# Sliding-window attention of a hybrid layer: the score scale applied where the mask is added, and four heads normalised by one product with a broadcast reciprocal

## Chip, cores and metric

The kernel runs on one core of a Trainium2 chip. The metric is the device time of one execution in microseconds (us); lower is better. The engines are named as in the profile: PE (TensorE, matrix products), PEld (its weight loads), DVE (VectorE), ACT (ScalarE), POOL (GpSimd) and SP (SyncE, which issues nearly all DMAs here).

## What is computed

One layer of a streaming encoder on 2048 tokens of 1024 columns: a token mixing block (one input projection whose columns feed 8 heads of sliding attention and 4 heads of a gated linear recurrence, HGRN2; one output projection), then cross-attention into 256 memory tokens, then a SwiGLU FFN. The change lies in the sliding attention alone:

```python
s = jnp.einsum('bnqhgd,bnkhd->bnhgqk', qc, kband).astype(jnp.float32) * (Dh ** -0.5)   # Dh = 64
s = jnp.where(valid[None, :, None, None, None, :], s, NEG_INF)
sink = ...                                # one learned logit for each head
p = jax.nn.softmax(jnp.concatenate([s, sink], axis=-1), axis=-1)[..., :L]
o = jnp.einsum('bnhgqk,bnkhd->bnqhgd', p.astype(v.dtype), vband)
```

A chunk of 64 queries reads its own chunk of keys and the two before it. The 8 query heads share 2 key heads, 4 and 4.

## The kernel before

All products run in 32-bit reduced form, each operand split into a high and a low part, so that a product is two or three matmuls. The work is staged: the input projection of the first 1024 tokens (up to about 255 us), then a stage of about 350 us in which three things are interleaved, then a passage of some 150 us that prepares the cross-attention weights (`fold_cross`) beside the second half of the recurrence, then the long products of the output projection, the cross-attention and the FFN.

The stage in the middle is the one that matters here. `mix` (line 194) advances generators in turn: `swa` (964, the sliding attention, 16 tiles of 128 tokens), `hgrn` (946, the recurrence) and `in_proj` (682, the input projection of the second 1024 tokens, one block of 128 columns at a step). What the generators emit is not the order of the engines: the kernel is built with a scheduler (`schedule_with_timeline_sim=True`) that reorders the whole instruction stream by its own forecast of durations and then fixes one queue for each engine. Each engine works through its queue in order, so an instruction that waits holds all that stand behind it. A changed instruction can therefore move others that the change doesn't touch.

For each tile, `swa_front` (754) does this. It loads the queries of 4 heads twice, into partitions 0 to 63 and 64 to 127 of `qd`; ACT makes `qs` with its scale (768) and DVE replaces the lower half by the remainder (769). Keys are split into `kh` and `kl` (779). A head's scores are two matmuls (803, 804) into a PSUM bank that holds two heads. One DVE instruction (808) adds the mask to the scores, writes the sum to `S` and leaves the row's minimum; ACT takes the exponential with that minimum and leaves the row's sum (812). For 4 heads together POOL adds the sink to the minimum (815), ACT takes its exponential (816), POOL adds it to the sums (818), DVE takes the reciprocal (820), and four DVE products, one for each head, multiply `S` by its column of the reciprocal (821 to 823). As the scores enter with a minus sign (the queries are scaled by -0.125), minima stand for maxima and the mask is +1e30.

`swa_back` (826) works one tile later: PE transposes `S` (837), ACT and DVE split the result into `pth` (841) and `ptl` (842), PE multiplies by the values (846, 847), ACT and DVE gather the halves into `ys` (850, 851), and `ys` is stored.

Some other lines take part in the argument. `in_cols` (690) loads a block of `w_in` columns into `raw`, splits it into `whi` and `wlo`, multiplies (156 to 158 into `psg`), ends a gate block with DVE (711) and stores `z` to `z_d` (721). The `z` tiles have two buffers. After the last block the same two buffers serve the prologue of `phases` (1317 to 1321): pieces of `w_out` are loaded into `z` and split into the resident tiles `T` by ACT (985) and DVE (988). `hgrn_front` (854) loads `k1`, `qq`, `kk`, `v` from `z_d`, and PE transposes `kk` (895) and `v` (900). `fold_cross` (272) transposes the memory tokens (124), and ACT and DVE write `mT` (126, 127) for the products that follow.

Of the kernel before, what the change touches and what calls it, by code (L numbers as in the profile page):

```python
# [11 lines left out]
F32 = mybir.dt.float32  # L12
F32R = mybir.dt.float32r
I32 = mybir.dt.int32
AF = mybir.ActivationFunctionType
ALU = mybir.AluOpType
AX = mybir.AxisListType

P = 128
T = 2048  # L20
D = 1024
M = 256
# [9 lines left out]
BIG = 1e30  # L32
# [4 lines left out]
def f32(ap):  # L37
    return ap.bitcast(F32)
# [10 lines left out]
class Layer:  # L49
# [345 lines left out]
    def zero_tiles(self):  # L395
        nc, ph = self.nc, self.hg

        self.wmask = self.sw.tile([P, M], F32, name="wmask")
        nc.vector.memset(self.wmask, 0.0)
        nc.vector.memset(self.wmask[0:64, 192:256], BIG)  # L400
        nc.vector.memset(self.wmask[64:128, 0:64], BIG)

        cm = self.io.tile([P, P], F32, tag="u", name="cm", bufs=2)
        nc.vector.memset(cm, 1.0)
        nc.gpsimd.affine_select(cm, cm, [[1, P]], ALU.is_ge, 0.0, base=0, channel_multiplier=-1)
        nc.vector.memset(cm[0:64, 64:128], 0.0)
        self.cmask = ph.tile([P, P], I32, name="cmask")
        nc.vector.tensor_copy(self.cmask, cm)

        self.atz = []  # L410
        for i in range(2):
            a = ph.tile([P, 4, P], F32, name=f"atz{i}")
            nc.gpsimd.memset(a, 0.0)
            self.atz.append(a)
        self.vst_prev = None
        self.W = ph.tile([P, 4, P], F32, tag="W", name="W0", bufs=2)
        nc.gpsimd.memset(self.W, 0.0)
# [336 lines left out]
    def swa_front(self, n, kinds):  # L754
        nc, ph = self.nc, self.sw
        t0 = n * P
        z = self.z_d
        nk = 2 if n else 1
        kinds = itertools.cycle(kinds)

        qs = []
        for g in range(2):
            qd = ph.tile([P, 4, P], F32, tag="qd", name=f"qd{n}_{g}", bufs=2)
            qsrc = z[g * 256:(g + 1) * 256, t0:t0 + P].rearrange("(h d) t -> d h t", d=64)
            self.load(qd[0:64], qsrc)
            self.load(qd[64:128], qsrc)
            q = ph.tile([P, 4, P], F32R, tag="qs", name=f"qs{n}_{g}", bufs=2)
            nc.scalar.activation(q, qd, AF.Copy, scale=-0.125)
            nc.vector.scalar_tensor_tensor(q[64:128], qd[64:128], -0.125, f32(q[64:128]), ALU.mult, ALU.subtract)
            qs.append(q)  # L770

        kr = ph.tile([P, 2, M], F32, tag="kr", name=f"kr{n}")
        kl = ph.tile([P, 2, M], F32R, tag="kl", name=f"kl{n}")
        kh = ph.tile([P, 2, M], F32R, tag="kh", name=f"kh{n}")
        o = M - nk * P
        ksrc = z[C_KA:C_VA, t0 + P - nk * P:t0 + P].rearrange("(g d) t -> d g t", d=64)
        self.load(kr[0:64, :, o:], ksrc)
        self.load(kr[64:128, :, o:], ksrc)
        self.split(kr[:, :, o:], kh[:, :, o:], kl[:, :, o:])

        vr = ph.tile([P, P], F32, tag="vr", name=f"vr{n}")
        self.load(vr, z[C_VA:C_QH, t0:t0 + P])
        pv = self.bank(next(kinds))
        nc.tensor.transpose(pv[:, 0:P], vr, self.ident)
        vst = ph.tile([P, 2, P], F32R, tag="vst", name=f"vst{n}", bufs=3)
        nc.scalar.activation(vst[:, 0, 0:64], pv[:, 0:64], AF.Copy)
        nc.scalar.activation(vst[:, 1, 64:128], pv[:, 64:128], AF.Copy)
        nc.vector.tensor_tensor(vst[:, 0, 64:128], pv[:, 0:64], f32(vst[:, 0, 0:64]), ALU.subtract)
        nc.vector.tensor_tensor(vst[:, 1, 0:64], pv[:, 64:128], f32(vst[:, 1, 64:128]), ALU.subtract)
        vs = [vst] if nk == 1 else [self.vst_prev, vst]  # L790
        self.vst_prev = vst

        S = []
        for g in range(2):
            mn = self.small("w_mn", 4)
            den = self.small("w_den", 4)
            for i2 in range(2):
                s = ph.tile([P, 2, M], F32, tag="S", name=f"S{n}_{g}{i2}", bufs=6)
                S.append(s)
                ps = self.bank(next(kinds))  # L800
                for r in range(2):
                    pr = ps[:, r * M + o:(r + 1) * M]
                    nc.tensor.matmul(pr, qs[g][:, 2 * i2 + r, :], kh[:, g, o:], start=True, stop=False)
                    nc.tensor.matmul(pr, qs[g][:, 2 * i2 + r, :], kl[:, g, o:], start=False, stop=True)
                for r in range(2):
                    i = 2 * i2 + r
                    h = 4 * g + i
                    nc.vector.tensor_tensor_reduce(  # L808
                        out=s[:, r, o:], in0=ps[:, r * M + o:(r + 1) * M], in1=self.wmask[:, o:],
                        op0=ALU.add, op1=ALU.min, scale=1.0, scalar=self.nsink[:, h:h + 1],  # L810
                        accum_out=mn[:, i:i + 1])
                    nc.scalar.activation(s[:, r, o:], s[:, r, o:], AF.Exp, bias=mn[:, i:i + 1], scale=-1.0,  # L812
                                         accum_out=den[:, i:i + 1])
            se = self.small("w_se", 4)
            nc.gpsimd.tensor_tensor(se, self.sink[:, 4 * g:4 * g + 4], mn, ALU.add)
            nc.scalar.activation(se, se, AF.Exp)
            dn = self.small("w_dn", 4)
            nc.gpsimd.tensor_tensor(dn, den, se, ALU.add)
            rd = self.small("w_rd", 4)
            nc.vector.reciprocal(rd, dn)  # L820
            for i in range(4):
                a = S[2 * g + i // 2][:, i % 2, o:]
                nc.vector.tensor_scalar_mul(a, a, rd[:, i:i + 1])
        return S, vs

    def swa_back(self, n, kinds, S, vs):
        nc, ph = self.nc, self.sw
        nk = len(vs)
        o = M - nk * P
        kinds = itertools.cycle(kinds)  # L830
        ys = ph.tile([P, 4, P], F32, tag="ys", name=f"ys{n}")
        for g in range(2):
            t = []
            for kb in range(nk):
                ps = self.bank(next(kinds))
                for i in range(4):
                    nc.tensor.transpose(ps[:, i * P:(i + 1) * P],  # L837
                                        S[2 * g + i // 2][:, i % 2, o + kb * P:o + (kb + 1) * P], self.ident)
                th = ph.tile([P, 512], F32R, tag="pth", name=f"pth{n}_{g}{kb}", bufs=3)
                tl = ph.tile([P, 512], F32R, tag="ptl", name=f"ptl{n}_{g}{kb}", bufs=2)  # L840
                nc.scalar.activation(th, ps, AF.Copy)
                nc.vector.tensor_tensor(tl, ps, f32(th), ALU.subtract)
                t.append((th, tl))
            ps = self.bank(next(kinds))
            for kb in range(nk):
                nc.tensor.matmul(ps, vs[kb][:, g, :], t[kb][0], start=(kb == 0), stop=False)
                nc.tensor.matmul(ps, vs[kb][:, g, :], t[kb][1], start=False, stop=(kb == nk - 1))
            a, c = (slice(0, 64), slice(64, 128)) if g == 0 else (slice(64, 128), slice(0, 64))
            pr = ps.rearrange("p (h t) -> p h t", h=4)
            nc.scalar.activation(ys[a], pr[c], AF.Copy)  # L850
            nc.vector.tensor_tensor(ys[a], pr[a], ys[a], ALU.add)
        self.store(self.y_d[n, :, 0:512], ys.rearrange("p k t -> p (k t)"))
# [902 lines left out]
```

## Time and profile before

| | |
|---|---|
| time, median of 3 runs | 2589.82 us (2588.64 to 2592.41) |
| span of the profiled execution, first to last instruction | 2585.7 us |
| median less that span | 4.1 us |
| PE busy | 2548.3 us of the span (99%) |
| DVE busy | 1747.9 us (68%) |
| ACT busy | 1261.0 us (49%) |
| POOL busy | 428.4 us (17%) |
| mean granted TensorE clock | 0.998 |

The profile is of one execution. Its span leaves out what lies before the first and after the last instruction; the 4.1 us is the distance from that span to the median of the timed runs. A matmul's busy time runs on past the start of the next (0.39 us long, started every 0.23 us), so that a PE that is "busy" may still lose a tenth of a microsecond here and there. The four 128x256 products of line 823 run from 285.6 to 605.2 us of the span, and all of the sliding attention lies between about 277 and 625 us.

### The profile page before, as it was taken

The page shows a single profiled execution, that of the slowest core. Times are in us where ns is not written, and L with a number is a line of the kernel's source. Part 1 is how long each engine was busy: PE and PEld are TensorE (multiplying, and loading weights), DVE is VectorE, ACT ScalarE, POOL GpSimd, SP SyncE. Part 2 cuts the span into 40 slices and gives each one's busy share as a digit, 9 for nine tenths or more (in the row PEclk, how much of TensorE's full clock was granted, in tenths as well). Part 3 has the DMA queues.
Part 4 walks back from the last instruction along what each step waited for, and adds up shares of the span by engine and source line. Part 5 has one row for each costly group of instructions (what it writes and reads, how often), then busy time and mean ns, then how long its engine had stood idle before and what let it go on. Part 6 is the DMA issues. An engine that isn't in the chain of part 4 may idle for free.

```text
span 2585.7 us, 34998 instructions
## 1 busy us (share of the span) xinstructions
PE 2548.3 (99%) x12371; PEld 2135.9 (83%) x12371; DVE 1747.9 (68%) x2759; ACT 1261.0 (49%) x2633; POOL 428.4 (17%) x612
## 2 busy tenths in 40 slices
PE   9999999999999999999999999999999999999998
PEld 8888888888988778888878888888888888888886
DVE  7785588986557778788876655576566556564656
ACT  5563466665555566465563333353333334443543
POOL 5231334321302232222300000000000000000022
PEclk9999999999999999999999999999999999999999
DMA  6445655855888886666963622253565444566888
GB/s 188 147 163 179 198 168 152 253 185 167 258 290 281 296 287 210 205 222 210 327 233 115 203 97 75 98 203 124 177 205 194 146 146 139 208 201 186 262 213 218
DMA packets 363663, 506.03 MB, mean 196 GB/s; under 512 B 20960, under 2 KB 249312, under 8 KB 363488
## 3 DMA queue, kind: packets, MB, share of 16 engines
q1 hardware_dynamic: 357440, 481.77, 56.5%
q0 software_dynamic: 6048, 22.02, 4.7%
q8 instruction: 97, 1.59, 0.2%
q14 instruction: 78, 0.64, 0.1%
HBM read 337.00 MB, written 166.72 MB: 195 GB/s over the span
## 4 chain that ended last, share of the span: by engine, by line
PE 83%; DMA 7%; DVE 4%; ACT 3%; issue 2%; POOL 1%; SPq 0%; DVEq 0%; POOLq 0%; ACTq 0%
PE psm L1122 23%; PE psm L1124 23%; PE psm L1123 22%; PE psg L156 2%; PE psg L157 2%; PE psg L158 2%; PE pss L1374 1%; DMA row<-y_d 1%; DMA raw<-in_wo_x_dram 1%; DMA u_d<-row 1%; DMA h1t_d<-row 1%; DMA row<-h_d 1%; ACT junk L1471 1%; ACT T L985 0%; PE pss L837 0%
## 5 line engine op out<-in xcount | busy, mean ns | idle before, releaser
L1122 PE MATMUL psm<-T,S 128*128 128x512 f32 x2695 | 1043.8, 391 | 11.0 <-ACT part L1137 6.5
L1123 PE MATMUL psm<-T,S 128*128 128x512 f32 x2695 | 1049.1, 390 | 2.1 <-DVE T L988 1.9
L1124 PE MATMUL psm<-T,S 128*128 128x512 f32 x2695 | 1038.9, 390 | 3.6 <-DVE S L988 3.6
L1122 PEld LDWEIGHTS psm<-T,S 128*128 128x128 f32 x2695 | 506.2, 188 | 120.3 <-ACT part L1137 7.0
L1124 PEld LDWEIGHTS psm<-T,S 128*128 128x128 f32 x2695 | 506.2, 188 | 110.4 <-DVE S L988 5.3
L1123 PEld LDWEIGHTS psm<-T,S 128*128 128x128 f32 x2695 | 506.5, 188 | 107.5 <-DVE T L988 4.1
L985 ACT ACTIVATE S<-sum 128x512 fp32r<-128x512 f32 (+1 forms) x314 | 188.7, 619 | 359.6 <-PE psm L1124 267.8
L988 DVE TENSOR_TENSOR S<-sraw,S 128x512 fp32r<-128x512 f32 (+1 forms) x319 | 217.0, 687 | 215.9 <-ACT S L985 201.8
L988 DVE TENSOR_TENSOR S<-sum,S 128x512 fp32r<-128x512 f32 (+1 forms) x372 | 249.7, 681 | 47.0 <-ACT S L985 31.8
L1137 ACT ACTIVATE part<-psm 128x512 f32<-128x512 f32 x273 | 161.7, 597 | 242.8 <-PE psm L1124 221.5
L985 ACT ACTIVATE S<-sraw 128x512 fp32r<-128x512 f32 (+1 forms) x272 | 167.4, 617 | 111.2 <-PE psm L1124 99.3
L1500 POOL DMA_DIRECT2D row<-y_d x28 | 25.7, 919 | 1111.4 <-DVE row L1686 1036.5
L988 DVE TENSOR_TENSOR T<-row,T 128x1024 fp32r<-128x1024 f32 (+1 forms) x120 | 141.3, 1192 | 60.9 <-ACT T L985 60.4
L1471 ACT ACTIVATE junk<-row 128x512 f32<-128x512 f32 x160 | 99.7, 625 | 60.5 <-DVE row L1493 30.0
L157 PE MATMUL psg<-u,whi 128*128 128x512 f32 x320 | 127.8, 399 | 0.0
L158 PE MATMUL psg<-u,wlo 128*128 128x512 f32 x320 | 127.1, 397 | 0.0
L156 PE MATMUL psg<-u,whi 128*128 128x512 f32 x320 | 127.1, 397 | 0.0
L985 ACT ACTIVATE T<-row 128x1024 fp32r<-128x1024 f32 x120 | 119.9, 1028 | 10.5 <-DMA row<-qk_s 3.5
L987 POOL TENSOR_SCALAR S<-sum 128x512 fp32r<-128x512 f32 x58 | 53.4, 921 | 294.6 <-PE psm L1124 237.2
L1637 DVE TENSOR_TENSOR row<-psm,part 128x512 f32<-128x512 f32 x66 | 43.7, 687 | 61.4 <-PE psm L1124 61.3
L1646 DVE TENSOR_TENSOR part<-psm,part 128x512 f32<-128x512 f32 x60 | 39.7, 687 | 62.4 <-PE psm L1124 62.2
L812 ACT ACTIVATE S<-S,w_mn 128x256 f32<-128x256 f32 (+1 forms) x128 | 63.1, 495 | 28.6 <-DVE w_mn L808 28.3
(363 smaller groups left out, 3679.1 us busy)
## 6 DMA issues: line engine op xcount, KB each, us to landing
sraw<-in_w_gate_dram SPq DMA_DIRECT2D x44, 512.0 KB, 3.7
sraw<-in_w_up_dram SPq DMA_DIRECT2D x44, 512.0 KB, 3.7
hid_d<-row SPq DMA_DIRECT2D x44, 512.0 KB, 2.7
h_d<-row SPq DMA_DIRECT2D x32, 512.0 KB, 4.8
y_d<-row SPq DMA_DIRECT2D x32, 512.0 KB, 3.3
sraw<-hid_d SPq DMA_DIRECT2D x32, 512.0 KB, 5.1
row<-y_d POOLq DMA_DIRECT2D x28, 512.0 KB, 7.1
sraw<-in_w_in_dram SPq DMA_DIRECT2D x44, 256.0 KB, 3.5
```

Source lines behind the costliest of these rows:

```text
L156: nc.tensor.matmul(ps, ah, bh, start=(i == 0), stop=False)
L157: nc.tensor.matmul(ps, ah, bl, start=False, stop=False)
L158: nc.tensor.matmul(ps, al, bh, start=False, stop=(i == n - 1))
L812: nc.scalar.activation(s[:, r, o:], s[:, r, o:], AF.Exp, bias=mn[:, i:i + 1], scale=-1.0, accum_out=den[:, i:i + 1])
L985: self.nc.scalar.activation(hi, raw, AF.Copy)
L987: self.nc.gpsimd.tensor_scalar(hi, raw, 1.0, 1.0, ALU.mult, ALU.mult)
L988: self.nc.vector.tensor_tensor(lo, raw, f32(hi), ALU.subtract)
L1122: nc.tensor.matmul(ps, s[:, 0, k, :], t[:, 0, k, :], start=st, stop=False, **kw)
L1123: nc.tensor.matmul(ps, s[:, 0, k, :], t[:, 1, k, :], start=False, stop=False, **kw)
L1124: nc.tensor.matmul(ps, s[:, 1, k, :], t[:, 0, k, :], start=False, stop=sp, **kw)
L1137: nc.scalar.activation(t, ps, AF.Copy)
L1471: self.nc.scalar.activation(junk, a, AF.Square, scale=float(D) ** -0.5, accum_out=to)
```

## The change

Three edits, all in the sliding attention:

- The queries are no longer scaled: `qs` is a plain copy, and its lower half is a plain subtraction (a tensor_tensor in place of a scalar_tensor_tensor). The mask becomes -1e30, and the instruction that adds it multiplies the sum by -0.125, with an argument that it has already (`scale`, 1.0 before).
- `S` is one tile of four heads with three buffers in place of tiles of two heads with six buffers; the bytes are the same.
- The four products of a group of heads with their columns of the reciprocal become one tensor_tensor of 128x1024 (128x512 in the first tile of tokens, which has half the keys), whose second operand is the 128x4 reciprocal repeated along the keys. There are 32 such groups.

```diff
         nc.vector.memset(self.wmask, 0.0)
-        nc.vector.memset(self.wmask[0:64, 192:256], BIG)
-        nc.vector.memset(self.wmask[64:128, 0:64], BIG)
+        nc.vector.memset(self.wmask[0:64, 192:256], -BIG)
+        nc.vector.memset(self.wmask[64:128, 0:64], -BIG)
...
             q = ph.tile([P, 4, P], F32R, tag="qs", name=f"qs{n}_{g}", bufs=2)
-            nc.scalar.activation(q, qd, AF.Copy, scale=-0.125)
-            nc.vector.scalar_tensor_tensor(q[64:128], qd[64:128], -0.125, f32(q[64:128]), ALU.mult, ALU.subtract)
+            nc.scalar.activation(q, qd, AF.Copy)
+            nc.vector.tensor_tensor(q[64:128], qd[64:128], f32(q[64:128]), ALU.subtract)
...
             den = self.small("w_den", 4)
+            s4 = ph.tile([P, 4, M], F32, tag="S", name=f"S{n}_{g}", bufs=3)
+            S.append(s4)
             for i2 in range(2):
-                s = ph.tile([P, 2, M], F32, tag="S", name=f"S{n}_{g}{i2}", bufs=6)
-                S.append(s)
+                s = s4[:, 2 * i2:2 * i2 + 2, :]
...
                     nc.vector.tensor_tensor_reduce(
                         out=s[:, r, o:], in0=ps[:, r * M + o:(r + 1) * M], in1=self.wmask[:, o:],
-                        op0=ALU.add, op1=ALU.min, scale=1.0, scalar=self.nsink[:, h:h + 1],
+                        op0=ALU.add, op1=ALU.min, scale=-0.125, scalar=self.nsink[:, h:h + 1],
                         accum_out=mn[:, i:i + 1])
...
             nc.vector.reciprocal(rd, dn)
-            for i in range(4):
-                a = S[2 * g + i // 2][:, i % 2, o:]
-                nc.vector.tensor_scalar_mul(a, a, rd[:, i:i + 1])
+            a = s4[:, :, o:]
+            nc.vector.tensor_tensor(a, a, rd.unsqueeze(2).broadcast_to([P, 4, nk * P]), ALU.mult)
...
                     nc.tensor.transpose(ps[:, i * P:(i + 1) * P],
-                                        S[2 * g + i // 2][:, i % 2, o + kb * P:o + (kb + 1) * P], self.ident)
+                                        S[g][:, i, o + kb * P:o + (kb + 1) * P], self.ident)
```

In the built program DVE's queue loses 96 instructions (128 products become 32); PE, ACT, POOL and SP keep their counts. The scheduler gives another order, too: on all five engines the queues differ from the second tile of the sliding attention on to the end of the passage after it. Before that they agree, and behind it too, but for a few neighbours that change places.

## Prediction

> **What bounds the kernel now.** I read the page first: its span, the line of PE in part 1, and the chain that ended last.
>
> ```profile
> span 2585.7 us, 34998 instructions
> PE 2548.3 (99%) x12371; PEld 2135.9 (83%) x12371; DVE 1747.9 (68%) x2759; ACT 1261.0 (49%) x2633; POOL 428.4 (17%) x612
> PE 83%; DMA 7%; DVE 4%; ACT 3%; issue 2%; POOL 1%; SPq 0%; DVEq 0%; POOLq 0%; ACTq 0%
> ```
>
> PE is busy 99% of the span and makes 83% of the chain; DVE makes 4% of it. The change leaves PE's 12371 matmuls as they are, and works on DVE. Whether DVE matters in the stage at hand is told by the busy time in stretches, then by PE's waits in the sliding attention (255 to 605 us) and in the passage behind it (605 to 650 us).
>
> ```profile
> core 0: us, PE busy (x) PEld busy (x) DVE busy (x) ACT busy (x) POOL busy (x), PEclk, DMA share, GB/s
> 255.00:605.00 350.00, 348.04 (x1927) 297.21 (x1926) 278.11 (x693) 207.18 (x606) 118.55 (x187) 1.00 0.63 189
> 605.00:650.00 45.00, 41.62 (x266) 37.54 (x265) 28.07 (x41) 24.84 (x46) 5.04 (x7) 0.96 0.69 194
> ```
> ```profile
> PE psh L847 <- DVE ptl L842: 0.9, 3, 0.5
> PE pss L803 <- DVE vst L789: 0.5, 1, 0.5
> PE pst L837 <- DVE w_mn L808: 0.2, 1, 0.2
> ```
> ```profile
> PE pst L900 <- DMA v<-z_d: 1.7, 1, 1.7
> PE psg L895 <- issue: 1.2, 1, 1.2
> PE pst L923 <- ACT atz L886: 0.5, 1, 0.5
> ```
>
> In the stage of the change PE is idle 350.00 - 348.04 = 2.0 us, of which it waited 0.9 + 0.5 + 0.2 = 1.6 us for DVE. That is all that a faster DVE can win there. In the 45 us behind it PE is idle 3.4 us and its clock is granted at 0.96, worth another 45 x 0.04 = 1.8 us; the largest wait is for a DMA, the load of `v`.
>
> **The change part by part.** First the product itself. These groups are from the view by line and shape within 255 to 605 us (count, busy us, mean ns); the last row is from the view of line 738, the tensor_tensor 128x1024 with a repeated operand that the kernel has already (min, median, max ns).
>
> ```profile
> L823 DVE TENSOR_SCALAR S<-S,w_rd 128x256 f32<-128x256 f32 x119 | 37.1, 374 | 1.3
> L823 DVE TENSOR_SCALAR S<-S,w_rd 128x128 f32<-128x128 f32 x8 | 2.5, 382 | 0.1
> L769 DVE SCALAR_TENSOR_TENSOR qs<-qd,qs 64x512 fp32r<-64x512 f32 x32 | 25.7, 804 | 10.2 <-ACT qs L768 9.4
> L842 DVE TENSOR_TENSOR ptl<-pst,pth 128x512 fp32r<-128x512 f32 x27 | 18.4, 680 | 3.6 <-PE pss L847 1.6 <-ACT pth L841 1.1 <-PE psg L158 1.0
> L738 DVE TENSOR_TENSOR u<-u,d_mid 128x1024 f32<-128x1024 f32 x4 | 4.9, 1217 | 0.0
> L738 DVE TENSOR_TENSOR pair<-pair,d_mid x4: 1211/1218/1628, 110.9 to 175.2; 128x1024 f32<-128x1024 f32 x4
> ```
>
> Removed: 127 of the 128 products, 37.1 + 2.5 = 39.6 us. Added: 30 products of 128x1024 and 2 of 128x512. By line 738's mean of 1.217 us and line 842's of 0.680 us that is 30 x 1.217 + 2 x 0.680 = 37.9 us; if all were as slow as line 738's slowest (1.628 us), 50.2 us. So DVE gains 1.7 us or loses up to 10.6 us over 345 us. I take -1.7 us, since the mean of one group of line 738 and the median of the other agree at 1.217 and 1.218 us.
>
> The last of the four old products ended 1.13 us after the first began (next fence, second row), so the group is ready 0.1 us later. No new wait appears: the reciprocal already needs the sums of all four heads, so the first old product too stood behind four exponentials. The transposes need all four heads anyway.
>
> The subtraction on line 769 keeps its shape and its two operands in SBUF; its time is bounded by line 842's 0.680 us and its own 0.804 us, a gain of 0 to 32 x 0.124 = 4.0 us on DVE; I take 0. The copy on ACT, the mask, and the scale in line 808 change a constant: 0. The three buffers of `S` hold the same three groups as the six did: 0.
>
> All this is on DVE, and PE waited 1.6 us for DVE in the stage. The cover is what stands between in PE's queue: the input projection's matmuls. In the built queue 8.1 us of PE work or more (by the matmuls' own starting distances) separates a group's last score from its first transpose before the change, and 11.6 us or more after it. So the direct part is worth between -1.6 us and, if PE's waits for DVE doubled, +1.6 us; I take 0.
>
> ```profile
> 300.15 1.39 DVE L823 TENSOR_SCALAR S<-S,w_rd 128x256 f32<-128x256 f32 x4
> 583.81 1.14 DVE L823 TENSOR_SCALAR S<-S,w_rd 128x256 f32<-128x256 f32 x4
> ```
> ```profile
> 300.00 0.62 POOL L987 TENSOR_SCALAR kh<-kr 128x512 fp32r<-128x512 f32 x1 [1.03 <-PE pss L804]
> ```
>
> Those are four old products beside a POOL instruction (1.39 us) and without one (1.14 us). The Trainium skill, page "SBUF — State Buffer", section "Who interferes with whom", says that DVE and GpSimd hold a shared pair of ports for a whole instruction, the later one blocked, and that a DVE instruction with two SBUF inputs contends with GpSimd's reads. By that rule the new product is no freer than the old ones, which the two rows bear out, and it holds POOL out for 1.2 us in one piece. That would put a price on DVE and POOL, which the rival below works out.
>
> **Second, the order.** This is where I see a cost. The chain that ended last, from 608 to 632 us (start, us, what), and then SP's, PE's and ACT's rows that belong to it:
>
> ```profile
> 606.66 0.44 PE pss L837 x4
> 608.91 0.25 PE psg L157
> 609.19 1.07 ACT whi L985
> 612.73 3.87 DMA z_d<-z
> 617.27 4.08 DMA z<-in_w_out_dram
> 621.43 1.07 ACT T L985
> 622.53 1.24 DVE T L988
> 623.78 0.61 SPq L75
> 624.45 5.09 DMA z<-in_w_out_dram
> 630.59 1.55 ACT mT L126 x3
> ```
> ```profile
> 625.10 0.59 SPq L75 DMA_DIRECT2D v<-z_d  x1
> ```
> ```profile
> 630.19 0.63 PE L900 MATMUL pst<-ident,v 128*128 128x128 f32 x4 [1.71 <-DMA v<-z_d]
> 630.65 0.82 PE L884 MATMUL psg<-qq,k 128*128 128x192 f32 x4
> 632.65 0.63 PE L895 MATMUL psg<-ident,kk 128*128 128x128 f32 x4 [1.18 <-issue]
> 633.77 0.49 PE L923 MATMUL pst<-vt,atz 128*128 128x128 f32 x2 [0.49 <-ACT atz L886]
> ```
>
> The end of a projection block releases ACT's `whi`, then a gate tile is finished and stored, its `z` buffer takes a piece of `w_out` (4.08 us), ACT and DVE split that, and only then does SP issue the next piece and, behind it, `v` for tile 9. PE wants that `v` at 628.5 us and gets it at 630.19. In the queues of the changed kernel three things differ.
>
> (a) The block that starts the chain ends earlier: 16 transposes (0.11 us each) and 4 matmuls of 512 columns (0.23 us) that stood ahead of its last matmul now stand behind it: 16 x 0.11 + 4 x 0.23 = 2.7 us earlier.
>
> (b) `v` for tile 9 now stands behind one more piece of `w_out` on SP, which waits for the split of the one before. The piece that was issued at 623.78 goes out at 621.1; it lands at 621.1 + 0.6 + 5.1 = 626.8; ACT 1.07 and DVE 1.24 give 629.2 with their gaps; one issue of 0.6 us gives `v` at 629.9 in place of 625.10; after the same 630.19 - 625.10 = 5.1 us, line 900 starts at 635.0 in place of 630.19: +4.8 us.
>
> (c) Given back: products of line 884 (0.65 us to the next start at full clock) and line 895 (0.44) that stood behind the wait now stand ahead of it, and their own waits of 1.18 and 0.49 us fall into the longer one: 2.8 us. Lost again: ACT now makes the four `mT` copies behind the squares of line 928, which need line 923's result. Three copies are 1.55 us, to which I add about 1.0 us for the squares and 0.6 us on DVE (estimates; a DVE instruction of 512 columns is 0.68 above); against 2.5 us of PE work that stands between, 0.7 us is left over.
>
> Sum of the order: +4.8 - 2.8 + 0.7 = +2.7 us. Its bounds: if `v` costs nothing more than before, -3.4 us (this passage's idle time gone) with -1.8 us for the clock; if nothing is given back and the clock is held low twice as long, 4.8 + 0.7 + 1.8 = +7.3 us, with up to 2 us more in the next passage.
>
> The whole: 0 + 2.7. Against the profiled span that is 2588.4 us; the median of the runs lies 4.1 us above that span, so 2589.8 + 2.7 = 2592.5 us.
>
> **The rivals.**
>
> *Slower by the order.* The mechanism is (b) at its full price: PE meets `v` late and nothing is given back, because the chain does not start 2.7 us early. For it: the late load is the largest wait there now, and every step of the chain is a row. Against it: the work moved ahead. It decides when `v` is issued later than about 631 us. Time: 2589.8 + 7.3 = 2597.1 us.
>
> *Slower by the shared port.* POOL is busy 118.55 of 350 us, 34%; if each of the 32 products then waits half of its own 1.2 us, that is 32 x 0.34 x 0.6 = 6.5 us on DVE and as much on POOL. For it: the row of 1.39 us. Against it: DVE's idle time in the stage is 72 us, PE's wait for it 1.6 us. It decides if all of it reaches PE: 2596.3 us. This is what the skill's rule above would give.
>
> *Faster.* The new order removes the waits: 2.0 us of the stage, 3.4 us behind it and 1.8 us of clock, together 7.2 us: 2582.6 us. For it: transposes keep more distance, and the chain starts earlier. Against it: one more `w_out` piece ahead of `v`.
>
> **How the numbers follow.** A measurement of this kernel can tell about 0.2% (5.2 us) from no change. Forecast, with its own range of 2587 to 2595 us: 0.47. Slower by the order 0.29, by the port 0.06, faster 0.18. So: faster by over 0.2% 0.18, within 0.2% 0.47, slower 0.35. The range of 8 in 10 goes from the faster rival, 2582.5, to the slower one and its 2 us in the next passage with a little room for the runs' own scatter of 2588.64 to 2592.41: 2601 us.
>
> **What would show it.** Right: 32 rows on line 823 of about 1.22 us (0.69 for two), DVE's sum on that line near 38 us, PE busy about 348 of 350 us in the stage, and the wait of line 900 for `v` grown from 1.7 us to 3 us or more. Wrong: products of 1.5 us or more; PE waiting for lines 823 or 842 by several us; `v` for tile 9 landing before PE reaches it; or a new wait in the rest of the stage, whose order I judged by the distances in the queues alone.

## The result, and the profile after

| | before | after |
|---|---|---|
| time, median of 6 runs each | 2591.93 us (2588.64 to 2594.0) | 2599.53 us (2597.02 to 2602.69) |
| ratio after / before, 95% interval | | 1.003 (1.0019 to 1.004) |
| span of the profiled execution | 2585.7 us | 2600.6 us |

The changed kernel is 7.6 us slower, 0.3%. The forecast was 2592.5 us and "within 0.2%"; the measured time is outside the likeliest case's own range (2587 to 2595 us) and inside the whole one. It was forecast as +2.7 us with 0.47 for "within 0.2%" and 0.35 for "slower": the way was right, the size was not, and the range held because it was wide. The profiled execution after took 2602.3 us in all, 1.7 us more than its span, and is one of the slowest of its six; the two profiled spans are 14.9 us apart, twice the medians, so a difference between two single profiles is read below only where it comes back in other runs.

The page of the changed kernel: its span, the line of PE in part 1, and the chain that ended last.

```profile
span 2600.6 us, 34912 instructions
PE 2551.2 (98%) x12371; PEld 2137.4 (82%) x12371; DVE 1750.0 (67%) x2663; ACT 1260.9 (48%) x2633; POOL 438.5 (17%) x612
PE 79%; DMA 8%; DVE 4%; ACT 3%; issue 2%; POOL 2%; SPq 1%; DVEq 0%; POOLq 0%; ACTq 0%
```

DVE's busy time has hardly moved (1747.9 and 1750.0 us) and POOL's has grown by 10 us; PE has lost a point of its share, and the chain of waits has given four points from PE to the others. Where PE lost it is told by the busy time in stretches, after, with the same columns as before:

```profile
255.00:605.00 350.00, 344.17 (x1913) 294.91 (x1912) 274.24 (x585) 204.09 (x595) 127.51 (x185) 1.00 0.65 189
605.00:650.00 45.00, 40.01 (x237) 35.00 (x236) 29.43 (x46) 23.74 (x51) 6.04 (x9) 0.96 0.63 165
650.00:715.00 65.00, 57.89 (x473) 55.72 (x473) 30.32 (x47) 30.83 (x82) 19.66 (x25) 1.00 0.84 235
```

and, before, the third stretch, which the prediction did not show:

```profile
650.00:715.00 65.00, 63.72 (x533) 62.77 (x532) 30.68 (x50) 33.58 (x96) 23.05 (x29) 1.00 0.82 255
```

PE's idle time (length less busy) in the stage is 5.8 us where it was 2.0; in 605 to 650 us 5.0 where it was 3.4; in 650 to 715 us 7.1 where it was 1.3. The groups of the changed lines on DVE in 255 to 650 us:

```profile
L823 DVE TENSOR_TENSOR S<-S,w_rd 128x1024 f32<-128x1024 f32 x30 | 37.9, 1268 | 1.5
L823 DVE TENSOR_TENSOR S<-S,w_rd 128x512 f32<-128x512 f32 x2 | 1.9, 960 | 0.2
L769 DVE TENSOR_TENSOR qs<-qd,qs 64x512 fp32r<-64x512 f32 x32 | 23.3, 732 | 8.9 <-ACT qs L768 8.0
```

The product itself is near what the prediction said (37.9 us): 32 rows with a sum of 39.8 us, against 37.4 + 2.5 us for the old ones in the same window. So DVE's time on it does not explain PE's new idle time. What PE waited for (total us, times, longest), in the stage and in 605 to 800 us:

```profile
PE pss L837 <- DVE vst L789: 1.7, 1, 1.7
PE pst L837 <- DVE ys L851: 0.9, 1, 0.9
PE psh L804 <- DVE sg L942: 0.8, 1, 0.8
PE pst L837 <- DVE w_mn L809: 0.7, 1, 0.7
PE pss L837 <- DVE w_mn L809: 0.6, 1, 0.6
```
```profile
PE pst L900 <- DVE on L933: 3.3, 1, 3.3
PE pst L884 <- ACT atz L886: 3.0, 1, 3.0
PE psg L884 <- POOL h_vv L930: 1.6, 1, 1.6
PE psh L156 <- ACT whi L985: 1.5, 1, 1.5
```

Only the two waits for line 809 (808 before), the instruction with the new scale, are for a line that the change touches, and with the old scale in the same order, in old_in_new_order below, they are longer (1.2 and 1.0 us). The two largest that came back in the other runs of this order have the same shape; the wait for line 933, 3.3 us here, is 0.4 and 1.0 us in two others. Late in the stage (first fence, DVE and then PE, start and us) DVE stands 6.74 us before a sum of `w_out` blocks whose load has not landed, and behind it stand the values `vst` for which PE's bank is held. In the passage (second fence, ACT; third, PE) ACT stands 3.52 us before the split of a `w_out` piece; the copy of `atz`, ready since DVE's line 885 (626.92 us, 0.43 us), stands behind it and two more, and PE waits 2.96 us.

```profile
527.93 1.22 DVE L1032 TENSOR_TENSOR u<-u,x 128x1024 f32<-128x1024 f32 x1 [6.74 <-DMA x<-in_w_out_dram]
```
```profile
629.80 1.06 ACT L985 ACTIVATE T<-z 128x1024 fp32r<-128x1024 f32 x1 [3.52 <-DMA z<-in_w_out_dram]
632.32 0.26 ACT L886 ACTIVATE atz<-pst 64x128 f32<-64x128 f32 x1
```
```profile
529.57 0.63 PE L837 MATMUL pss<-ident,S 128*128 128x128 f32 x4 [1.69 <-DVE vst L789]
632.63 1.05 PE L884 MATMUL pst<-qq,k 128*128 128x192 f32 x4 [2.96 <-ACT atz L886]
637.73 0.60 PE L900 MATMUL pst<-ident,v 128*128 128x128 f32 x4
```

The last row is the place at which the prediction expected the wait, line 900 for `v` of tile 9: it starts at 637.73 us and waits for nothing, since PE comes late anyway.

### The profile page after: what moved, and what is told of

The parts are those of the page before. It is cut to its first block, busy times and chain, and to the rows that moved or that the text cites. A ratio compares the mean times of both kernels' runs of the same rounds, so it can differ in the third digit from the quotient of the medians.

```text
span 2600.6 us, 34912 instructions
## 1 busy us (share of the span) xinstructions
PE 2551.2 (98%) x12371; PEld 2137.4 (82%) x12371; DVE 1750.0 (67%) x2663; ACT 1260.9 (48%) x2633; POOL 438.5 (17%) x612
## 3 DMA queue, kind: packets, MB, share of 16 engines
q8 instruction: 97, 1.59, 0.3%
## 4 chain that ended last, share of the span: by engine, by line
PE 79%; DMA 8%; DVE 4%; ACT 3%; issue 2%; POOL 2%; SPq 1%; DVEq 0%; POOLq 0%; ACTq 0%
PE psm L1122 22%; PE psm L1124 22%; PE psm L1123 22%; PE psg L156 1%; PE psg L157 1%; PE psg L158 1%; PE pss L1374 1%; DMA row<-y_d 1%; DMA u_d<-row 1%; DMA kk<-z_d 1%; SPq L75 1%; ACT T L985 0%; DMA row<-d_s 0%; DMA qd<-z_d 0%; DMA raw<-in_wv_x_dram 0%
## 5 line engine op out<-in xcount | busy, mean ns | idle before, releaser
L1646 DVE TENSOR_TENSOR part<-psm,part 128x512 f32<-128x512 f32 x60 | 39.7, 687 | 60.4 <-PE psm L1124 60.2
```

## The experiments

Theory when the runs began: **order**. The change costs nothing where it is made; the scheduler, given other instructions, wrote other queues, and these make PE wait. Rival: **product**. The new instruction (1.27 us in one piece, POOL 9 us longer busy) costs the time itself. Each run was timed together with the kernel before, whose median lay between 2590.0 and 2592.2 us; ratio and interval are against those times.

### The two orders with the two sets of instructions

The queue of each engine of a built kernel can be written out and held: an edge between each instruction and the next on its engine, with no wait for its end, leaves the scheduler no choice. `QUEUES` holds the places of the instructions in the order of the other kernel:

```diff
+def held(tc):
...
+    ins = list(tc.nc.cur_bb.bb.instructions)
+    info = mybir.DependencyInfo(mybir.DependencyClass.NoSync, mybir.DependencyReason.DATA)
+    for q in QUEUES:
...
+        for a, b in zip(at, at[1:]):
+            tc.add_manual_dep(ins[b], ins[a].name, info, reason="queue")
...
         Layer(tc, I, out).run()
+        held(tc)
```

The changed kernel so held in the order of before:

> The changed kernel's instructions, with the queues of all five engines written out in the order of the kernel before (each new product stands where the last of its four old products stood). Theory 'order': all of the loss comes with the order of the queues, so this kernel takes the time of before, 2592 us (2589 to 2595), and PE's idle time in 605 to 650 us of the span is back at 3.4 us. Rival 'product': the new product itself (1.27 us in the mean, POOL busy 9 us longer in the stage) costs the time, so it stays at 2599.5 us (2597 to 2602) in any order. Both in part would give a time between 2594 and 2598 us.

The kernel before held in the order of the changed one:

> The instructions of the kernel before, with the queues of all five engines written out in the order of the changed kernel (the four old products stand together where the new one stood). Theory 'order': 2599.5 us (2597 to 2602), with line 884 waiting about 3 us for line 886's copy near 632 us of the span. Rival 'product': 2592 us (2589 to 2595).

Measured: new_in_old_order 2591.96 us, ratio 1.0002 (0.9993 to 1.0012); old_in_new_order 2601.33 us, ratio 1.0034 (1.0022 to 1.0046). All of the loss comes with the order, whoever's instructions run in it; in the old order the change costs 0.3 us, within 0.1%. "Product" falls.

The two halves of the change by themselves give the same two orders without any help. Only the scale (the kernel before with the change's edits of the mask, of `qs` and of this argument):

```diff
-                        op0=ALU.add, op1=ALU.min, scale=1.0, scalar=self.nsink[:, h:h + 1],
+                        op0=ALU.add, op1=ALU.min, scale=-0.125, scalar=self.nsink[:, h:h + 1],
```

> Of the change only the scale: q is not scaled, the mask is negative, line 808 scales by -0.125, and line 769 is a tensor_tensor; the tiles S and the four products stay. Its queues stand in the order of before. Theories 'order' and 'product' both give the time of before, 2592 us (2589 to 2595). A third, 'scale': the shorter subtraction (0.732 against 0.804 us in the mean, 32 of them, 2.3 us of DVE) reaches the end, which gives 2589.6 us.

Only the tile and the product (the changed kernel with the old mask, the old scales and the old line 769):

```diff
-            nc.scalar.activation(q, qd, AF.Copy)
-            nc.vector.tensor_tensor(q[64:128], qd[64:128], f32(q[64:128]), ALU.subtract)
+            nc.scalar.activation(q, qd, AF.Copy, scale=-0.125)
+            nc.vector.scalar_tensor_tensor(q[64:128], qd[64:128], -0.125, f32(q[64:128]), ALU.mult, ALU.subtract)
...
-                        op0=ALU.add, op1=ALU.min, scale=-0.125, scalar=self.nsink[:, h:h + 1],
+                        op0=ALU.add, op1=ALU.min, scale=1.0, scalar=self.nsink[:, h:h + 1],
```

> Of the change only the tile of four heads and the one product; q is scaled, and line 769 stays a scalar_tensor_tensor. Its queues stand in the order of the changed kernel. Theories 'order' and 'product' both give 2599.5 us (2597 to 2602); 'scale' gives 2.3 us more than the changed kernel, 2601.8 us.

Measured: scale_only 2593.74 us, 1.0005 (0.9997 to 1.0014); product_only 2602.73 us, 1.0034 (1.0021 to 1.0048). The scale leaves order and time alone; the tile with its product brings the new order and the whole loss. The four kernels also part the cost of an instruction from that of its surroundings. Line 769 in scale_only (a tensor_tensor, old order), then in product_only (a scalar_tensor_tensor, new order):

```profile
L769 DVE TENSOR_TENSOR qs<-qd,qs 64x512 fp32r<-64x512 f32 x32 | 26.4, 825 | 10.5 <-ACT qs L768 9.7
```
```profile
L769 DVE SCALAR_TENSOR_TENSOR qs<-qd,qs 64x512 fp32r<-64x512 f32 x32 | 23.4, 734 | 9.2 <-ACT qs L768 8.4
```

Its fall from 804 to 732 ns is a matter of order, not of the operation. And POOL's busy time (fifth pair) in the stage, in new_in_old_order and in old_in_new_order:

```profile
255.00:605.00 350.00, 346.40 (x1917) 295.77 (x1916) 272.39 (x580) 204.11 (x591) 124.34 (x183) 1.00 0.65 192
```
```profile
255.00:605.00 350.00, 344.04 (x1909) 294.75 (x1908) 273.79 (x673) 203.48 (x593) 122.58 (x184) 1.00 0.65 189
```

The new product adds 124.34 - 118.55 = 5.8 us to POOL in the old order and 127.51 - 122.58 = 4.9 us in the new one. Other profiles agree: in the old order POOL is busy 116.46 us in scale_only, with the old product, and 123.16 us in late_part_new, with the new one. That is the size of what the port rival reckoned for POOL, 6.5 us, and it does not reach the end: new_in_old_order takes the time of before.

### Which part of the order

At about 595 us both orders have issued exactly the same instructions, so that they can be joined there, in the changed kernel with its queues held (the packed queues are told in words here):

```diff
 late_part_new
-QUEUES: the changed order
+QUEUES: the order of before up to kt8 (897), the changed order behind it
 late_part_old
-QUEUES: the changed order
+QUEUES: the changed order up to kt8 (897), the order of before behind it
```

> The changed kernel's instructions; all queues in the order of before up to a point at about 595 us at which both orders have issued the same set of instructions (line 897's copy kt8 is the last), and in the changed kernel's order behind it. By PE's lost time (its starting distances beyond the shortest ones) in the six profiles so far, the new order loses 16.7 us in the mean between 585 and 715 us, the old one 10.0, and 5.1 against 2.7 us between 520 and 585. Theory 'two places': 2591.6 + 6.7 = 2598.3 us. Rival 'passage alone': 2599.5 us. Rival 'stage alone': 2592 us.

> The counterpart: the changed kernel's order up to the same point at about 595 us, the order of before behind it. Theory 'two places': 2591.6 + 2.4 = 2594 us, with the transposes of line 837 still waiting some 3 us near 529 to 540 us, and no 3 us wait of line 884 near 630 us. Rival 'passage alone': 2591.6 us. Rival 'stage alone': 2599.5 us.

("Lost time" there is worked out from all PE records of a trace: for each matmul the distance to the start of the next, less that distance at the fastest quarter of its form.) Measured: late_part_new 2597.37 us, 1.002 (1.0009 to 1.0031), 5.1 us above before; late_part_old 2594.88 us, 1.0006 (0.9996 to 1.0016), 2.6 us above by the medians and 1.6 by the ratio, with an interval that takes in no change. Together that is some 7 to 8 us, near the whole. "Stage alone" falls; the times by themselves don't part "two places" from "passage alone". The windows of late_part_new, then of late_part_old, say the same:

```profile
605.00:650.00 45.00, 39.71 (x228) 35.12 (x228) 27.75 (x44) 22.79 (x49) 5.85 (x9) 0.92 0.67 174
650.00:715.00 65.00, 60.99 (x499) 58.65 (x498) 30.86 (x48) 33.19 (x93) 20.76 (x27) 1.00 0.78 236
```
```profile
605.00:650.00 45.00, 41.46 (x257) 36.33 (x256) 29.65 (x52) 25.91 (x58) 5.79 (x11) 1.00 0.59 171
650.00:715.00 65.00, 63.51 (x526) 62.40 (x526) 33.90 (x54) 34.28 (x98) 22.95 (x29) 1.00 0.85 260
```

PE's idle time by order, from the windows of eight profiles:

| order in the stage | idle us, 255 to 605 | order behind it | idle us, 605 to 715 |
|---|---|---|---|
| old: before, scale_only, new_in_old_order, late_part_new | 2.0, 3.3, 3.6, 3.3 | old: before, scale_only, new_in_old_order, late_part_old | 4.7, 5.3, 6.0, 5.0 |
| new: after, product_only, old_in_new_order, late_part_old | 5.8, 5.9, 6.0, 7.1 | new: after, product_only, old_in_new_order, late_part_new | 12.1, 9.4, 7.6, 9.3 |

The means differ by 3.1 us in the stage and by 4.4 us behind it, 7.5 us in all.

These windows are fixed in time, though the executions stand up to 6 us apart (in new_in_old_order already when the sliding attention begins), and idle time is not all that is lost. Measured by the work instead, between two matmuls that have the same work ahead of them in both orders, the two places part clearly. From the 1480th of PE's 12371 records (at 307 to 313 us) to the 3065th (590 to 596 us) the four kernels with the old order take 282.5 to 284.0 us, those with the new one 284.9 to 285.6. From there to the 4200th (746 to 758 us) it is 155.3 to 158.3 us in the old order and 161.8 to 165.8 in the new. The means differ by 1.7 and by 6.9 us. So both places lose time, and most of it is lost in the passage. Part of what idle time leaves out there is the clock: in 605 to 650 us it is granted at 0.96, 1.00, 1.00 and 1.00 in the old order and at 0.96, 0.96, 0.92 and 0.92 in the new. Reckoned as in the prediction, 45 us times the difference of the means (0.99 and 0.94), that is some 2 us, an estimate.

### One wait at a time

In the passage, the wait of 2.96 us for `atz` was taken away first, in the changed kernel with its queues held. On ACT three copies pass the split of the second piece; in `act_and_v_moved` SP's load of `v` also passes the third piece:

```diff
 ACT
+ atz0 (886), ys15 (850), vt8 (902)
  T<-z_977 (985)
  whi (985), z (706)
- atz0 (886), ys15 (850), vt8 (902)
 SP, in act_and_v_moved
+ v for tile 9
  z_1003
- v for tile 9
```

> The changed kernel with its queues held, but on ACT three short copies (line 886 atz0, line 850 ys15, line 902 vt8) moved ahead of the split of the second w_out piece (line 985, T), which waits for its load. Theory 'head of the line': line 884's wait of 3.0 us goes, and with it 3 us of the time: 2596.5 us. Rival 'next wait': v for tile 9 lands at about 637.7 us of the span whatever ACT does, so line 900 waits for it in place of line 884 and the time stays at 2599.5 us.

> As act_moved, and on SP the load of v for tile 9 stands ahead of the third w_out piece (z_1003) that it followed. 'Head of the line': the same as act_moved, 2596.5 us. 'Next wait': act_moved gains nothing, and here both waits go: 2596.5 us. If w_out's next pieces bind instead (the third piece's split stands ahead of line 902's next copy on ACT), neither gains more than 1 us.

Measured: 2599.43 us, 1.0027 (1.0019 to 1.0036), and 2600.34 us, 1.0022 (1.0012 to 1.0033). Nothing gained by either. PE's rows of act_moved show why:

```profile
629.55 0.89 PE L884 MATMUL pst<-qq,k 128*128 128x192 f32 x4 [1.41 <-ACT T L985]
632.92 0.92 PE L884 MATMUL psg<-qq,k 128*128 128x192 f32 x4 [1.59 <-DVE z L711]
641.43 1.62 PE L884 MATMUL psg<-qq,k 128*128 128x192 f32 x4 [2.89 <-DMA kk<-z_d]
```

Line 884 starts 3.1 us earlier than in the changed kernel (629.55, 632.63), 1.5 us of it because this execution is that much further on (its first `w_out` piece is issued at 616.26, that of the changed kernel at 617.78). Its next product waits for a bank that line 711 holds, which on DVE stands behind the other half of the same split and the split of `wlo`; the one after that waits for the recurrence's loads. "Next wait" was right that another takes the place, and wrong about which: it was not `v`.

So the whole preparation of `w_out` was queued behind the first tiles of the recurrence, in the changed kernel and in the one before:

```diff
-                    if 2 <= i < 10:
-                        next(phases)
+                    if i == 2:
+                        with self.queued(*(self.traced(e) for e in (mybir.EngineType.SP, mybir.EngineType.Activation, mybir.EngineType.DVE))):
+                            next(phases)
+                    elif i < 10 and i > 2:
+                        next(phases)
```

> The changed kernel, and the first step of the preparation of w_out (loads z, line 985/988 splits T) is queued behind what is already written for SP, ACT and DVE, so that its pieces stand behind v for tiles 9 and 10 and behind the first recurrence tiles; up to about 600 us all queues are as in the changed kernel. Theory 'side work at the head of the queues': the waits of lines 884, 900 and 923 between 605 and 715 us go; PE's lost time of 585 to 715 us falls from 15 to 18 us to 8 us or less, and the time from 2599.5 to 2590 to 2593 us. Rival 'the recurrence's own chain': the waits belong to the chain of lines 884, 886, 911 and 923, and stay: 2599.5 us. Third: the pieces come too late for the matmuls behind 780 us, and the gain is given back there.

> The same edit on the kernel before, whose order up to about 600 us stays. 'Side work at the head of the queues': the waits of 1.7, 1.2 and 0.5 us in 605 to 650 us and the lower clock there go, 2592.2 - 3 = 2589 us (2586 to 2591). 'The recurrence's own chain': 2592 us.

Measured: 2600.81 us, 1.0042 (1.003 to 1.0054), and 2594.17 us, 1.0016 (1.0005 to 1.0027). No gain in the one, a loss of about 4 us in the other. The windows of w_out_behind, whose line numbers are higher by 3:

```profile
605.00:650.00 45.00, 43.58 (x275) 38.60 (x274) 28.75 (x52) 24.00 (x57) 7.51 (x12) 1.00 0.49 140
650.00:715.00 65.00, 55.66 (x441) 54.38 (x440) 31.45 (x47) 31.69 (x81) 17.58 (x23) 0.92 0.86 243
```

PE's idle time in the first stretch fell from 5.0 to 1.4 us, as the theory said, and rose in the second to 9.3 us. In before_w_out_behind it is the same: 3.4 us became 0.2, and 1.3 became 6.3. The pieces that had used a quieter time of the DMA engines (share 0.49 now, 0.63 before the move) now come when the recurrence and the memory weights load too (0.86), and they block again, 47 us later and for longer (6.17 us on ACT, 3.52 in the changed kernel). That the busier DMA engines make the wait longer was not tested. ACT's row, DVE's, PE's:

```profile
677.16 1.06 ACT L988 ACTIVATE T<-z 128x1024 fp32r<-128x1024 f32 x1 [6.17 <-DMA z<-in_w_out_dram]
```
```profile
678.25 1.68 DVE L991 TENSOR_TENSOR T<-z,T 128x1024 fp32r<-128x1024 f32 x1 [6.29 <-ACT T L988]
```
```profile
683.49 1.08 PE L898 MATMUL psg<-ident,kk 128*128 128x128 f32 x4 [4.84 <-issue]
```

The last wait has no name in the view; in the built queue line 898 waits for DVE, whose line 916 (682.71 us, 0.68 us) frees that kind of bank and stands behind the split.

For the end of the stage one instruction was moved on DVE, the sum that waited 6.74 us:

```diff
 DVE
- u<-u,x (1032)
  vst11 (788, 789), ys9 (851), S11_0 (809) twice
+ u<-u,x (1032)
  qs12 (769)
```

> The changed kernel with its queues held, but on DVE one sum of w_out blocks (line 1032, u plus x), which waited 6.7 us for its load at 521 to 528 us, stands behind the four products of line 809 for S11_0 and no longer ahead of lines 788 and 789. Theory 'side work at the head of the queues' for the end of the stage: line 837's wait of 1.7 us at 529 us goes, and with it the time: 2597.8 us, perhaps 2597. Rival: another wait takes its place, as in act_moved, and the time stays at 2599.5 us.

Measured: 2600.34 us, 1.004 (1.0025 to 1.0055). The wait of 1.69 us is gone, PE's busy time in the stage is 345.26 us where it was 344.17, and the time is not better. By PE's records the stage takes 284.0 us, 1.2 us less than the mean of the new order, and the passage 163.9 us, as in the new order. The wait for `atz` there, 3.0 us in the changed kernel, has grown to 4.4, as the view of PE's waits in 605 to 650 us of dve_moved shows.

```profile
PE pst L884 <- ACT atz L886: 4.4, 1, 4.4
PE psg L884 <- DMA kk<-z_d: 2.1, 1, 2.1
```

### All waits of 605 to 650 us at once

Last, what stood ahead of the recurrence on ACT, DVE and PE was moved together, in late_part_new (on DVE the partners of ACT's copies move with them):

```diff
 ACT
+ atz0 (886), ys15 (850), vt8 (902), z (706)
  T<-z_977 (985), whi (985)
- z (706), atz0 (886), ys15 (850), vt8 (902)
+ mT, three of four (126)
  T<-z_1003 (985), atz1 (886), kt9 (897), vt9 (902)
+ mT, the fourth (126)
  squares of on8 (928)
- mT, all four (126)
 PE
+ 48 products on mT (156 to 158)
  products of line 884 for tile 10
- 48 products on mT (156 to 158)
```

> late_part_new (2597.4 us) with every wait of 605 to 650 us addressed at once: on ACT atz0, ys15, vt8 and line 706's z stand ahead of the second w_out piece, and three of the four mT copies of line 126 ahead of the third; on DVE the partners of these are moved with them (lines 711, 851, 127); on PE the first 48 matmuls of the memory projection (lines 156 to 158 on mT) stand ahead of line 884 for tile 10 and no longer behind it. SP and POOL stay in the new order. Theory 'stack of waits': act_moved gained nothing because the next waits took the place of the first one, so that all must go together; here PE's idle time in 605 to 650 us falls from 5.3 us to 1.5 us or less and the time to 2593 us (2591 to 2594.5). Rival 'limited by the loads': the tiles of the recurrence come no faster than SP's loads of k, qq and kk let them, so idle time only moves behind 650 us, and the time stays at 2597 us (2596 to 2599).

Measured: 2597.61 us, 1.0029 (1.0019 to 1.0039), where late_part_new had 1.002. "Stack of waits" falls: no gain. PE's rows, then SP's and DVE's, of three_moves:

```profile
628.00 0.89 PE L884 MATMUL pst<-qq,k 128*128 128x192 f32 x4 [1.23 <-DMA k<-z_d]
632.73 0.63 PE L895 MATMUL psg<-ident,kk 128*128 128x128 f32 x4 [1.86 <-issue]
635.09 1.12 PE L900 MATMUL pst<-ident,v 128*128 128x128 f32 x4 [1.74 <-DMA v<-z_d]
```
```profile
630.47 0.37 SPq L75 DMA_DIRECT2D z<-in_w_out_dram  x1
630.89 0.46 SPq L75 DMA_DIRECT2D v<-z_d  x1
```
```profile
629.11 1.33 DVE L988 TENSOR_TENSOR T<-z,T 128x1024 fp32r<-128x1024 f32 x1
630.37 1.21 DVE L988 TENSOR_TENSOR wlo<-raw,whi 128x1024 fp32r<-128x1024 f32 x1
631.95 0.68 DVE L913 TENSOR_TENSOR W<-psg,W 128x512 f32<-128x512 f32 x1
```

The waits for `atz` and `kk` are gone, and three others are there. Two are for loads: `k` for tile 9, and `v` for tile 9, issued right behind the third piece and landing 1.74 us late. This is the wait that the prediction named, at last in sight. The largest, 1.86 us before line 895, has no name in the view. It ends 0.1 us after DVE's line 913, which reads a bank of the kind that line 895 writes and stands behind both splits of line 988 on DVE; that this is what PE waited for is argued, not shown. So the engines' own blocks were probably not all gone. "Limited by the loads" gave 2596 to 2599 us and has the time, but loads are not all that is left, and the idle time did not move behind 650 us: 45.00 - 38.23 = 6.8 us of it are still in 605 to 650 us, where late_part_new had 5.3.

## Why the prediction was right or wrong, point by point

**The product on DVE: right in effect, a little off in price.** Forecast -1.7 us on DVE (37.9 for 39.6 us); measured 39.8 against 39.9 us, nothing. The mean of the large ones was 1.268 us and not 1.217, of the small ones 0.960 and not 0.680 (the median of all 32 is 1.224). That none of it reaches the end was right, and shown: 1.0002 in the old order.

**Line 769, the scale, the mask: right.** Taken at 0; scale_only 1.0005 (0.9997 to 1.0014), and the operation's median is the same (0.690 and 0.689 us).

**The port rival: near the mark for POOL, wrong for DVE and for the end.** 4.9 to 5.8 us more on POOL against 6.5 reckoned; on DVE the products took 39.8 us, where 37.9 + 6.5 were reckoned; the time in the old order shows none of it. The rule of the Trainium skill, page "SBUF — State Buffer", section "Who interferes with whom" (a tensor_tensor with both inputs in SBUF contends with GpSimd's reads), agrees with POOL's rows; that the time would follow, which I had hung on it, did not come.

**The order, the stage: wrong.** "No new wait appears" and the 0 for the stage were judged by PE's own queue, by the distance between a group's last score and its first transpose. That distance did grow, as said. But the stage lost 1.7 us by PE's records, with 3.1 us more idle time. The largest wait, 1.7 us, came about because DVE's queue now had a sum with a late load (line 1032) ahead of what PE needed: it goes when that sum is moved. The other waits of the stage were not taken apart. The prediction's last sentence named a new wait in the stage as a thing that would make it wrong; it had no price in the sum.

**The order, the passage: the place and the late pieces right, the sum too small.** Forecast +2.7 us, measured 5.1 us by the times (late_part_new) and 6.9 by PE's records. The steps can be measured from the 3065th record on, in three kernels with the old order throughout (before, scale_only, new_in_old_order) and three with the new one (after, product_only, old_in_new_order).

- Step (a), the chain starts 2.7 us earlier. The first piece is issued 27.0 to 27.1 us after that record in the old order and 25.0 to 25.2 in the new, 1.9 us earlier. The stage had lost about as much, so that counted from the span's start nothing is left of it (616.61 us before, 617.78 after).
- Step (b), +4.8 us. `v` is issued 35.5 to 35.6 us after the record in the old order and 39.7 to 40.3 in the new, and line 900 starts at 40.0 to 40.8 and at 45.1 to 45.5, so the size is right. The wait is not: line 900 waits for nothing in the changed kernel, since a late piece blocked ACT and DVE first and PE with them. That the two ways to be late have the same length is in part luck.
- Step (c), 2.8 us given back, is the step that failed. The products put ahead of line 900 were meant to cover the wait for `v`; the first of them waited itself, 2.96 us for `atz`, and behind line 900 the next tile waited another 1.6 to 1.9 us. Nothing came back: PE is some 5 us behind at line 900, 6 at the 3600th record and 7 at the 4200th.

Without (c) the sum is 4.8 + 0.7 = +5.5 us. The rival "slower by the order" adds 1.8 us for a lower clock, which the new order does have, and comes to +7.3 us. That this is near the whole 7.6 us is luck, as the stage has a part in it for which the rival had no term. Its condition, `v` issued later than about 631 us, held in the changed kernel (632.56 us).

**The base.** The 4.1 us between span and median were taken to lie around the span. All six runs after show 1.7 us there; the rest says that the profiled execution before was a fast one (2585.7 + 1.7 = 2587.4 us, below all six timed ones). The forecast as a difference doesn't depend on it. The time does: 2592.5 us stands on a base of 2589.8, and the six runs before gave 2591.9.

**What stays open.** Which waits make up the loss of the passage is not settled: four edits (act_moved, act_and_v_moved, w_out_behind, three_moves) took away the waits that were largest, and each time others came up within 50 us. That the loads set the time in the end is one reading of three_moves, beside a block on DVE that was left in it, and no kernel that gains shows it: the moves of three_moves together with the loads of `k` and `v` ahead of the pieces were not tried. Nor is it shown what in the order of before makes its passage shorter; no repair came back to its time. No version beat the kernel before.

## What to carry to other kernels

Where a scheduler writes the queues, a local edit has two prices, that of the instruction and that of the new order; hold the queues of the one kernel for the instructions of the other, both ways, and the times tell the two apart before any theory of the instruction is needed. To judge an order, look on every engine's queue for instructions that wait for a DMA and see what stands behind them; the distances on the bound engine's own queue didn't show it here. That is a place to look and not a cure: no repair built on it gained. And a wait that is largest in the list is not worth its length: taking away 3.0 us, 1.7 us, and then the two waits of late_part_new together (2.8 and 2.5 us) gained nothing that the times show, as other waits grew or came up in their place.

## What the runs showed of the hardware

- A scalar_tensor_tensor of 64x512 and a tensor_tensor of the same shape take the same (0.690 and 0.689 us at the median); the mean of this line, 0.73 or 0.83 us, went with the order of the queues and not with the operation.
- A long tensor_tensor and a POOL instruction beside it can both stretch. One product took 1.77 us (1.22 at the median) and the POOL instruction that began within it 1.59 us (0.62 for the same form at 643.61 us of the same span):

```profile
536.17 1.77 DVE L823 TENSOR_TENSOR S<-S,w_rd 128x1024 f32<-128x1024 f32 x1
```
```profile
536.82 1.59 POOL L877 TENSOR_TENSOR qq<-qq,G 128x256 f32<-128x256 f32 x1
```

- A low granted clock stood beside PE's longest idle time: in 680 to 695 us of w_out_behind PE was idle 6.0 of 15 us and the row's clock is 0.66. Which of the two comes first no run here shows.

```profile
680.00:695.00 15.00, 9.01 (x54) 8.64 (x55) 7.92 (x12) 7.38 (x19) 3.91 (x5) 0.66 0.87 245
```
